# A segment-mean kernel: shorter look-ahead, a look in one slot, and a tail moved off GpSimd

## Chip, cores and metric

The kernel runs on one core of a Trainium2 chip. The metric is device time in microseconds, the median of several executions. The profile is one execution taken by the hardware profiler; its span is about 2 us shorter than the time.

## The reference

```python
def setup_inputs():
    n, num_segments = 10_000_000, 10000
    return {"data": np.random.randn(n).astype(np.float32),
            "segment_ids": np.sort(np.random.randint(0, num_segments, n))}

def reference(data, segment_ids):
    ...
    np.add.at(sums, segment_ids, data)
    np.add.at(counts, segment_ids, 1)
    return sums / np.maximum(counts, 1)
```

The ids are sorted, and a segment has about 1000 elements. The draw is fixed.

## The kernel before

Each of the 128 partitions takes 78125 consecutive elements, as 98 rows of 800. A row holds at most one segment boundary. For a group of four or five rows there is first a *look*: probes (every 160th id) tell the id at the start of each row (`V`), whether the row holds a boundary (`BT`), and where. A GpSimd gather fetches the 159 ids around the boundary, ScalarE adds them up, and that gives the exact split point `KK`. For every row ScalarE then forms the row's total `T` and VectorE the part before the split, `A` (the "split", one operation over 800 elements). `V`, `BT`, `KK`, `A` and `B` lie in one tile, which the profile calls `q_118` or `q`.

The program is written as slots: slot r issues the total and the split of row r, then whatever small work `put` has placed there, for a look (`first_look`, five steps) one step a slot. `X_PROBE`, `X_DATA`, `X_LOOK` and `X_SUM` are in rows ahead.

```python
X_PROBE = 18; X_DATA = 26; X_LOOK = 16; X_SUM = 7     # rows ahead
R1 = 94; R2 = NR + 4; C1 = 58; ON_ACT = 89

def first_look(g):                       # s1 to s5; s5 starts the gathers
    def s1():
        ...
        nc.vector.tensor_copy(out=V[:, a:e], in_=pr32[:, a:e, 0])

def keys(a, b):                          # s1: base1; s2: key = id - base; s3: dm
    def s2():
        nc.vector.tensor_scalar(out=KEY[:, PAD + a : PAD + b], in0=V[:, a:b],
            scalar1=base1[:, 0:1], scalar2=None, op0=ALU.subtract)

def windows_hold(r, n, o1, o2):          # part of the guard
    # s1, s2: j2 = (row - 1.625 - 1.25 * KEY) ** 2
    # s3: o1 = (j2 > 3.625**2) * BT      row with a boundary, outside its window
    ...

def verdict():                           # sum of all guard columns, over all partitions
    # s1: reduce, matmul with ones;  s2: badi = sum != 0

def finish():
    for f in sums(R1, R2, False): f()
    nc.vector.tensor_tensor(out=add[:, :, 0:m], in0=pk, in1=..FF.., op=ALU.mult)
    nc.vector.tensor_reduce(out=OUT[:, C1:NO], in_=add, axis=AX.X, op=ALU.add)
    ...  # four output DMAs
    with tc.If(verdict_reg[0] > 0):
        general_path(...)                # any sorted or unsorted ids, very slow

# the schedule (cut)
for g in range(HEAD, NG):
    put(max(bounds[g] - X_LOOK, 0), first_look(g))     # one step a slot
put(26, extend())
put(31, keys(0, 48))                                   # s2 in slot 32
put(36, ext_rows())
...
put(91, counts(66, R2), 3)
put(93, sums(66, R1), 4)
t, p = table(12, NT1 // 4, g), place(36, NO, g)        # g: on GpSimd
put(93, t[:1]); put(95, t[1:] + p[:1], 2); put(96, p[1:])
put(94, verdict())
after[96].append(lambda: verdict_reg.append(nc.values_load(badi[0:1, 0:1], ...)))
```

To turn rows into outputs, the kernel compares `KEY` (id - base) with column numbers, but only in windows of 12 rows for four columns, which fits ids that advance evenly. The guard tests that each boundary lies in its window. If one does not, the whole result is computed again by `general_path`, column by column. Rows from `R1` on skip the windows: they are compared with all columns from `C1` on and added by products (`pk`).

Of the kernel before, what the change touches and what calls it, by code (L numbers as in the profile page):

```python
# [9 lines left out]
FP32 = mybir.dt.float32  # L10
# [7 lines left out]
P = 128  # L18
# [8 lines left out]
NX = NR + E  # L27
BIG = float(1 << 24)
GROUPS = [4] + [5] * 18 + [4]
X_PROBE = 18  # L30
X_DATA = 26
X_LOOK = 16
X_SUM = 7
RING = 28
NO = 79
SHIFT = 6
ND = 2 * SHIFT + 1
NT1 = 92
R1 = 94
R2 = NR + 4  # L40
C1 = 58
ON_ACT = 89



# [68 lines left out]
def kernel(  # L114
# [116 lines left out]
    def first_look(g):  # L231

        a, b = bounds[g], bounds[g + 1]
        n = b - a
        eq = fpool.tile([P, n, K - 1], FP32, name="eq", bufs=3)
        jc = fpool.tile([P, n], FP32, name="jc", bufs=3)
        pos = fpool.tile([P, n], FP32, name="pos", bufs=3)
        last = b == NR

        def s1():  # L240
            if last:
                nc.vector.tensor_copy(out=pr32[:, NR - 1, 2 * (K - 1) : 2 * K], in_=snt32)
                nc.vector.tensor_copy(out=vend, in_=snt32[:, 0:1])
                nc.vector.tensor_copy(out=V[:, NR : NR + 1], in_=snt32[:, 0:1])
            in1b, in0b = bass.broadcast_tensor_aps(pr32[:, a:b, 0:1], pr32[:, a:b, 2 : 2 * K : 2])
            nc.vector.tensor_tensor(out=eq, in0=in0b, in1=in1b, op=ALU.is_equal)  # L246
            e = b if last else b + 1
            nc.vector.tensor_copy(out=V[:, a:e], in_=pr32[:, a:e, 0])  # L248

        def s2():  # L250
            nc.vector.tensor_reduce(out=jc, in_=eq, axis=AX.X, op=ALU.add)  # L251
            nc.vector.tensor_sub(out=BT[:, a:b], in0=V[:, a + 1 : b + 1], in1=V[:, a:b])  # L252

        def s3():
            nc.vector.tensor_scalar(  # L255
                out=ST[:, a:b], in0=jc, scalar1=float(S), scalar2=float(1 + W),
                op0=ALU.mult, op1=ALU.add,
            )
            nc.vector.tensor_scalar(  # L259
                out=NB[:, a:b], in0=BT[:, a:b], scalar1=1.0, scalar2=None, op0=ALU.not_equal  # L260
            )
            if last:
                nc.vector.tensor_scalar(
                    out=ST[:, NR - 1 : NR], in0=ST[:, NR - 1 : NR], scalar1=float(LAST), scalar2=None,
                    op0=ALU.min,
                )

        def s4():
            nc.vector.tensor_add(out=pos, in0=ST[:, a:b], in1=wb[:, a:b])  # L269
            nc.vector.scalar_tensor_tensor(  # L270
                out=QQ[:, a:b], in0=V[:, a:b], scalar=float(W), in1=ST[:, a:b],
                op0=ALU.mult, op1=ALU.add,
            )

        def s5():
            nc.vector.scalar_tensor_tensor(  # L276
                out=IDX[:, a:b], in0=NB[:, a:b], scalar=BIG, in1=pos, op0=ALU.mult, op1=ALU.add
            )

            nc.vector.scalar_tensor_tensor(  # L280
                out=QQ[:, a:b], in0=NB[:, a:b], scalar=-64.0 * BIG, in1=QQ[:, a:b], op0=ALU.mult,
                op1=ALU.add,
            )
            gather(g)

        return [s1, s2, s3, s4, s5]
# [16 lines left out]
        )  # L303

    def second_look(a, b):
        def s0():
            c = a
            while c < b:
                s = c % RING
                e = min(b, c - s + RING)  # L310
                nc.vector.tensor_reduce(  # L311
                    out=GS[:, c:e], in_=gt32[:, s : s + e - c, 0 : 2 * W : 2], axis=AX.X, op=ALU.add
                )
                c = e

        def s1():
            nc.vector.tensor_sub(out=KK[:, a:b], in0=QQ[:, a:b], in1=GS[:, a:b])  # L317

        def s2():
            nc.vector.tensor_mul(out=KK[:, a:b], in0=KK[:, a:b], in1=BT[:, a:b])  # L320

        return [s1] if a < ON_ACT else [s0, s1, s2]

    def total(r):
        n = min(L, D - r * L)
# [30 lines left out]
    KL = cpool.tile([P, R2 - R1], FP32, name="KL")  # L356
    pk = cpool.tile([P, NO - C1, R2 - R1], FP32, name="pk")
    add = cpool.tile([P, NO - C1, R2 - R1 + 1], FP32, name="add")
    OUT = cpool.tile([P, NO], FP32, name="OUT")
    nc.vector.memset(RF, 0.0)  # L360
    nc.vector.memset(CS[:, 0:1], 0.0)
# [14 lines left out]
    def view(ap, dims):  # L376
        return bass.AP(ap.tensor, ap.offset, [list(ap.ap[0])] + dims)
# [33 lines left out]
    def keys(a, b):  # L411
        def s1():
            if a == 0:
                nc.vector.tensor_add(out=base1, in0=V[:, 0:1], in1=pin)

        def s2():
            nc.vector.tensor_scalar(
                out=KEY[:, PAD + a : PAD + b], in0=V[:, a:b], scalar1=base1[:, 0:1], scalar2=None,
                op0=ALU.subtract,
            )  # L420
            if a == 0:
                nc.vector.tensor_sub(out=delta, in0=sp, in1=base1)

        def s3():
            if a == 0:
                nc.vector.tensor_scalar(
                    out=dm, in0=jj[:, 0:ND], scalar1=delta[:, 0:1], scalar2=None, op0=ALU.is_equal
                )

        return [s1, s2, s3]  # L430
# [137 lines left out]

        return [s1, s2, s3, s4, s5, s6, s7]

    def sums(a, b, weigh=True):
        def s1():
            c = min(b, NR)
            nc.vector.tensor_sub(out=B[:, a:c], in0=T[:, a:c], in1=A[:, a:c])  # L574

        def s2():
            nc.vector.tensor_tensor_scan(  # L577
                out=CS[:, a + 1 : b + 1], data0=NB[:, a:b], data1=B[:, a:b], initial=CS[:, a : a + 1],
                op0=ALU.mult, op1=ALU.add,
            )  # L580

        def s3():
            nc.vector.tensor_add(out=FF[:, a:b], in0=A[:, a:b], in1=CS[:, a:b])  # L583

        def s4():
            nc.vector.tensor_mul(out=RF[:, PAD + a : PAD + b], in0=FF[:, a:b], in1=RB[:, a:b])

        return [s1, s2, s3, s4] if weigh else [s1, s2, s3]
# [55 lines left out]
    def select(m0, m1, e):  # L644
        def s1():
            equal(e, sel[:, m0:m1], windows(KEY, m0, m1),
                  view(jj[:, 4 * m0 : 4 * m0 + 1], [[4, m1 - m0], [1, 4], [0, 12]]))

        return [s1]
# [33 lines left out]
    def pick():  # L683

        n, m = NO - C1, R2 - R1

        def s1():
            nc.gpsimd.tensor_scalar(
                out=KL, in0=V[:, R1:R2], scalar1=sp[:, 0:1], scalar2=None, op0=ALU.subtract
            )  # L690
            equal(nc.gpsimd, pk, view(KL[:, 0:1], [[0, n], [1, m]]),
                  view(jj[:, C1 : C1 + 1], [[1, n], [0, m]]))

        def s2():
            nc.gpsimd.tensor_tensor(  # L695
                out=pk, in0=pk, in1=view(RB[:, R1 : R1 + 1], [[0, n], [1, m]]), op=ALU.mult
            )

        return [s1, s2]

    def finish():
        n, m = NO - C1, R2 - R1
        for f in sums(R1, R2, False):
            f()
        nc.vector.tensor_tensor(
            out=add[:, :, 0:m], in0=pk, in1=view(FF[:, R1 : R1 + 1], [[0, n], [1, m]]), op=ALU.mult
        )
        nc.vector.tensor_reduce(out=OUT[:, C1:NO], in_=add, axis=AX.X, op=ALU.add)
        for i, (src, dst) in enumerate(own_outputs(OUT, out2d[0:1, :])):
            (nc.scalar if i % 2 else nc.sync).dma_start(out=dst, in_=src)  # L710
        with tc.If(verdict_reg[0] > 0):
            general_path(tc, fpool, ppool, data, segment_ids, out2d, iota)
# [11 lines left out]
    def put(r, steps, every=1):  # L724
        for i, f in enumerate(steps):
            after[r + i // every].append(f)
# [3 lines left out]
            after[-1].append(f)  # L730
    after[-1] += second_look(0, GROUPS[0])
    for a, b in zip(bounds[1:], bounds[2:]):
        put(a - 2 if a < ON_ACT else a - 3 if b < NR else a - 4, second_look(a, b))
    for g in range(HEAD, NG):
        put(max(bounds[g] - X_LOOK, 0), first_look(g))

    v, g = nc.vector, nc.gpsimd
    verdict_reg = []
# [8 lines left out]
    put(64, counts(48, 66), 2)  # L747
    put(67, sums(48, 66) + table(8, 12, v) + place(0, 36, v), 2)
    put(60, check(), 2)
    last_look = bounds[NG - 1] - X_LOOK + 4  # L750
    put(last_look + 1, keys(MID, NX)[1:] + check_late())
    put(last_look + 2, select(12, NT1 // 4, g))
    put(last_look + 2, pick()[:1])
    put(last_look + 2, [lambda: nc.sync.dma_start(out=out2d[0:SHIFT, :].rearrange("n u -> u n"), in_=tab[0:1, 0:SHIFT])])
    put(91, counts(66, R2), 3)
    put(93, pick()[1:])
    put(93, sums(66, R1), 4)
    t, p = table(12, NT1 // 4, g), place(36, NO, g)
    put(93, t[:1])
    put(95, t[1:] + p[:1], 2)  # L760
    put(96, p[1:])
    put(94, verdict())
    after[96].append(lambda: verdict_reg.append(nc.values_load(badi[0:1, 0:1], min_val=0, max_val=1)))
    assert max(after) <= NR - 1

    pnext = 0
# [62 lines left out]
```

## Time and profile before

| | before |
|---|---|
| time, median of 3 | 197.04 us |
| last data landed (the trace's DMA packet records) | 178.0 us |
| VectorE starts the split of row 84, its last wait for data | 165.22 us |
| VectorE's last operation ends | 188.94 us |
| end of the span | 194.885 us |

Here are three parts of the page of the kernel before: the span, the busy time of each engine, and the busy tenths in 40 slices of 4.9 us.

```profile
span 194.9 us, 1624 instructions
PE 1.6 (1%) x6; PEld 1.4 (1%) x6; DVE 139.9 (72%) x541; ACT 138.1 (71%) x393; POOL 108.0 (55%) x121
...
DVE  6535197874775867495967686967999679899960
DMA  6999999999999999999999999999999999993000
```

The DMA queues are full until about 178 us. After that VectorE (DVE) works off a backlog. The last slices hold only the output and the end of the program. The split of row 84 is the last at which VectorE waits for data (columns as explained below):

```profile
165.22 1.05 DVE L333 SCALAR_TENSOR_TENSOR junk_v<-iota,q_118,data_t 128x800 bf16<-128x800 f32 x1 [0.46 <-DMA data_t<-in_data_dram]
```

The timeline shows the end of the kernel before. Columns: start in us, duration in us, engine, line, operation, output <- inputs; in brackets the idle time before it and what ended it.

```profile
169.17 0.98 DVE L311 TENSOR_REDUCE GS<-GT 128x5 f32<-128x795 int32 x1 [0.47 <-ACT junk_a L300]
175.20 0.82 DVE L311 TENSOR_REDUCE GS<-GT 128x4 f32<-128x636 int32 x1
184.44 0.15 DVE L528 TENSOR_SCALAR badi<-badp 128x1 int32<-128x1 f32 x1
184.60 1.33 POOL L668 TENSOR_TENSOR shf<-tab,dm 128x559 f32<-128x559 f32 x1 [1.45 <-DVE badi L528]
185.96 0.45 DVE L675 TENSOR_REDUCE OUT<-shf 128x22 f32<-128x286 f32 x1 [0.41 <-POOL shf L668]
188.59 0.35 DVE L708 TENSOR_REDUCE OUT<-add 128x21 f32<-128x189 f32 x1
188.97 1.48 SPq L710 DMA_DIRECT2D out_dram<-OUT  x2
```

The first two operations add up the gathered ids of rows 89 to 97 a second time: ScalarE has 98 such sums in the page, one for every row. The last GpSimd operation (POOL) ends at 185.9 us. VectorE is done at 188.94 us, and the span ends 5.95 us later.

### The profile page before, as it was taken

Reading aid. Unit: us, or ns where it says so; the run is one execution under the profiler, and the core shown is the slowest. Engines: PE = TensorE matmul, PEld = TensorE weight load, DVE = VectorE, ACT = ScalarE, POOL = GpSimd, SP = SyncE. Lnnn points to the kernel's source line nnn. Section 1 sums busy time; section 2 is a strip of 40 time slices with the busy share of each in tenths; the row PEclk is TensorE's granted clock in tenths of the full one; section 3 lists DMA queues with packets and bytes.
Section 4 is the critical chain, followed back from the end, with each engine's and each line's share of the span. In section 5 each row is a group of like instructions: output and inputs, shape, how many; then the busy total and the mean of one; then the engine's idle time right before and its main releaser. Section 6 shows DMA issues by size and latency. Waiting matters only on the chain.

```text
span 194.9 us, 1624 instructions
## 1 busy us (share of the span) xinstructions
PE 1.6 (1%) x6; PEld 1.4 (1%) x6; DVE 139.9 (72%) x541; ACT 138.1 (71%) x393; POOL 108.0 (55%) x121
## 2 busy tenths in 40 slices
PE   0000000000000200000000000000000000000100
PEld 0000000000000100000000000000000000000100
DVE  6535197874775867495967686967999679899960
ACT  0043398985999998595968686866978779999310
POOL 5487737775467573746456373737383674850410
DMA  6999999999999999999999999999999999993000
GB/s 82 127 107 323 244 400 246 385 246 403 202 336 318 372 246 260 360 279 345 176 389 252 367 210 405 238 317 264 380 261 274 396 401 400 399 403 133 2 2 9
DMA packets 75141, 53.40 MB, mean 274 GB/s; under 512 B 65601, under 2 KB 65684, under 8 KB 75127
## 3 DMA queue, kind: packets, MB, share of 16 engines
q1 hardware_dynamic: 70251, 40.54, 73.9%
q0 software_dynamic: 4704, 12.74, 21.7%
q14 instruction: 14, 0.11, 0.2%
q10 hardware_dynamic: 172, 0.00, 0.1%
HBM read 56.46 MB, written 0.04 MB: 290 GB/s over the span
## 4 chain that ended last, share of the span: by engine, by line
DMA 31%; SPq 30%; issue 14%; DVE 10%; ACT 10%; POOL 3%; POOLq 0%; DVEq 0%; ACTq 0%
SPq L162 24%; DMA data_t<-in_data_dram 23%; DMA GT<-in_segment_ids_dram,IDX 7%; SPq L154 6%; ACT junk_a L328 5%; DVE junk_v L333 5%; ACT junk_a L300 4%; POOL GT L290 2%; POOL shf L668 1%; DVE CS L577 1%; DVE tab L658 0%; DVE GS L311 0%; DVE ct L559 0%; DVE FF L583 0%; DVE q_118 L574 0%
## 5 line engine op out<-in xcount | busy, mean ns | idle before, releaser
L290 POOL DMA_INDIRECT GT<-in_segment_ids_dram,IDX x98 | 98.3, 1003 | 66.2 <-ACT junk_a L300 31.2
L333 DVE SCALAR_TENSOR_TENSOR junk_v<-iota,q_118,data_t 128x800 bf16<-128x800 f32 x98 | 102.1, 1042 | 26.8 <-DMA data_t<-in_data_dram 23.7
L328 ACT ACTIVATE junk_a<-data_t 128x800 bf16<-128x800 f32 x98 | 85.0, 867 | 22.5 <-DMA data_t<-in_data_dram 13.6
L300 ACT ACTIVATE junk_a<-GT 128x159 bf16<-128x159 int32 x98 | 34.0, 346 | 15.6 <-DMA GT<-in_segment_ids_dram,IDX 8.3
L300 ACT ACTIVATION_READ_ACCUMULATOR junk_a<-GT 128x1 f32 x98 | 18.3, 187 | 0.0
L328 ACT ACTIVATION_READ_ACCUMULATOR junk_a<-data_t 128x1 f32 x98 | 18.2, 186 | 0.0
L317 DVE TENSOR_TENSOR q_118<-QQ,GS 128x5 f32<-128x5 f32 (+1 forms) x20 | 3.2, 160 | 15.9 <-issue 11.6
L300 ACT ACT_TABLE_LOAD x1 | 1.3, 1283 | 9.6 <-DVE q_118 L252 9.6
L333 DVE DVE_READ_ACCUMULATOR junk_v<-iota,q_118,data_t 128x1 f32 x98 | 8.1, 83 | 0.0
L246 DVE TENSOR_TENSOR eq<-pr 128x20 f32<-128x20 int32 (+1 forms) x20 | 3.5, 175 | 2.6 <-DMA pr<-in_segment_ids_dram 2.6
L695 POOL TENSOR_TENSOR pk<-pk,RB 128x168 f32<-128x168 f32 x1 | 0.5, 507 | 7.2 <-DVE q_118 L574 7.2
L248 DVE CAST q_118<-pr 128x6 f32<-128x6 int32 (+2 forms) x20 | 3.7, 183 | 0.0
L259 DVE TENSOR_SCALAR NB<-q_118 128x5 f32<-128x5 f32 (+1 forms) x20 | 3.5, 176 | 0.0
L255 DVE TENSOR_SCALAR ST<-jc 128x5 f32<-128x5 f32 (+1 forms) x20 | 3.5, 174 | 0.0
L251 DVE TENSOR_REDUCE jc<-eq 128x5 f32<-128x20 f32 (+1 forms) x20 | 3.4, 171 | 0.0
L269 DVE TENSOR_TENSOR pos<-ST,wb 128x5 f32<-128x5 f32 (+1 forms) x20 | 3.3, 167 | 0.0
L276 DVE SCALAR_TENSOR_TENSOR IDX<-NB,pos 128x5 int32<-128x5 f32 (+1 forms) x20 | 3.2, 158 | 0.0
L280 DVE SCALAR_TENSOR_TENSOR QQ<-NB,QQ 128x5 f32<-128x5 f32 (+1 forms) x20 | 3.1, 157 | 0.0
L270 DVE SCALAR_TENSOR_TENSOR QQ<-q_118,ST 128x5 f32<-128x5 f32 (+1 forms) x20 | 3.1, 156 | 0.0
L252 DVE TENSOR_TENSOR q_118<-q_118 128x5 f32<-128x5 f32 (+1 forms) x20 | 3.1, 156 | 0.0
L311 DVE TENSOR_REDUCE GS<-GT 128x5 f32<-128x795 int32 (+1 forms) x2 | 1.8, 899 | 0.6 <-ACT junk_a L300 0.5
L668 POOL TENSOR_TENSOR shf<-tab,dm 128x559 f32<-128x559 f32 x1 | 1.3, 1332 | 1.4 <-DVE badi L528 1.4
(110 smaller groups left out, 41.8 us busy)
## 6 DMA issues: line engine op xcount, KB each, us to landing
data_t<-in_data_dram SPq DMA_DIRECT2D x48, 800.0 KB
GT<-in_segment_ids_dram,IDX POOLq DMA_INDIRECT x98
pr<-in_segment_ids_dram SPq DMA_DIRECT2D x18, 25.0 KB
data_t<-in_data_dram SPq DMA_DIRECT2D x1, 400.0 KB
data_t<-in_data_dram SPq DMA_DIRECT2D x1, 262.5 KB
out_dram<-OUT SPq DMA_DIRECT2D x1, 36.6 KB
pr<-in_segment_ids_dram SPq DMA_DIRECT2D x1, 21.0 KB
pr<-in_segment_ids_dram SPq DMA_DIRECT2D x1, 18.0 KB
```

Of the source, the lines that this page charges most:

```text
L154: nc.sync.dma_start(out=pr_flat[:, a:b], in_=ids_p[:, a * S : (b - 1) * S + 1 : S])
L162: nc.sync.dma_start(out=d[:, 0 : c - a], in_=data_p[:, a:c])
L246: nc.vector.tensor_tensor(out=eq, in0=in0b, in1=in1b, op=ALU.is_equal)
L248: nc.vector.tensor_copy(out=V[:, a:e], in_=pr32[:, a:e, 0])
L251: nc.vector.tensor_reduce(out=jc, in_=eq, axis=AX.X, op=ALU.add)
L255: nc.vector.tensor_scalar(out=ST[:, a:b], in0=jc, scalar1=float(S), scalar2=float(1 + W), op0=ALU.mult, op1=ALU.add,)
L259: nc.vector.tensor_scalar(out=NB[:, a:b], in0=BT[:, a:b], scalar1=1.0, scalar2=None, op0=ALU.not_equal)
L269: nc.vector.tensor_add(out=pos, in0=ST[:, a:b], in1=wb[:, a:b])
L290: nc.gpsimd.indirect_dma_start(out=GT[:, r % RING, :], out_offset=None, in_=ids2d[:], in_offset=bass.IndirectOffsetOnAxis(ap=IDX[:, r : r ...
L300: nc.scalar.activation(out=junk_a[:, 0:W], in_=gt32[:, r % RING, 0 : 2 * W : 2], func=ACT.Relu, accum_out=GS[:, r : r + 1],)
L328: nc.scalar.activation(out=junk_a[:, 0:n], in_=d, func=ACT.Copy, accum_out=t)
L333: nc.vector.scalar_tensor_tensor(out=junk_v[:, 0:n], in0=iota[:, 0:n], scalar=KK[:, r : r + 1], in1=d, op0=ALU.is_lt, op1=ALU.mult, accum_ ...
```

## The change

The intent is to look later, so that fewer probes come before the first data, to take the second summing and the closing products off VectorE's end, and to let GpSimd finish early. Its core (cut: helper bodies and some schedule lines are left out):

```diff
-X_PROBE = 18
+X_PROBE = 13
-X_LOOK = 16
-X_SUM = 7
+X_LOOK = 11
+X_SUM = 6
-R1 = 94
+R1 = 84
-C1 = 58
-ON_ACT = 89
+C1 = 50
@@ second_look: the tensor_reduce over GT and the product with BT are gone @@
@@ pick: product with RB on VectorE; wq = sum of the last columns; wp = pk[last row] - wq @@
@@ all_but_last (new): sums, product and reduction of rows 84.. without the last row @@
@@ finish @@
+        nc.vector.scalar_tensor_tensor(
+            out=most, in0=wq, scalar=T[:, r : r + 1], in1=most, op0=ALU.mult, op1=ALU.add)
+        nc.vector.scalar_tensor_tensor(
+            out=OUT[:, C1:NO], in0=wp, scalar=A[:, r : r + 1], in1=most, op0=ALU.mult, op1=ALU.add)
@@ schedule @@
-        put(max(bounds[g] - X_LOOK, 0), first_look(g))
+        put(max(bounds[g] - X_LOOK, 0), first_look(g), 5)
-    put(last_look + 2, select(12, NT1 // 4, g))
+    put(last_look + 2, select(12, NT1 // 4, v))
-    put(91, counts(66, R2), 3)
-    put(93, sums(66, R1), 4)
-    t, p = table(12, NT1 // 4, g), place(36, NO, g)
-    put(94, verdict())
+    put(R1, counts(66, R1), 4)
+    put(R1 + 2, sums(66, R1), 4)
+    t, p = table(12, NT1 // 4, v), place(36, NO, g)
+    put(R1 + 3, t + p[:1])
+    put(R1 + 4, verdict())          # read at slot R1 + 6
+    put(NR - 4, counts(R1, R2), 4)
+    put(NR - 3, pick()[1:], 2)
+    put(NR - 2, all_but_last(), 5)
```

More of the change, by code (lines that the diff above doesn't have):

```diff
@@ L305, in second_look @@
     def second_look(a, b):
-        def s0():
-            c = a
-            while c < b:
-                s = c % RING
-                e = min(b, c - s + RING)
-                nc.vector.tensor_reduce(
-                    out=GS[:, c:e], in_=gt32[:, s : s + e - c, 0 : 2 * W : 2], axis=AX.X, op=ALU.add
-                )
-                c = e
         def s1():
             nc.vector.tensor_sub(out=KK[:, a:b], in0=QQ[:, a:b], in1=GS[:, a:b])
-        def s2():
-            nc.vector.tensor_mul(out=KK[:, a:b], in0=KK[:, a:b], in1=BT[:, a:b])
-        return [s1] if a < ON_ACT else [s0, s1, s2]
+        return [s1]
     def total(r):
@@ L358 @@
     add = cpool.tile([P, NO - C1, R2 - R1 + 1], FP32, name="add")
+    wq = cpool.tile([P, NO - C1], FP32, name="wq")
+    wp = cpool.tile([P, NO - C1], FP32, name="wp")
+    most = cpool.tile([P, NO - C1], FP32, name="most")
     OUT = cpool.tile([P, NO], FP32, name="OUT")
@@ L569, in counts, with sums @@
         return [s1, s2, s3, s4, s5, s6, s7]
-    def sums(a, b, weigh=True):
+    def sums(a, b, weigh=True, upto=NR):
         def s1():
-            c = min(b, NR)
+            c = min(b, upto)
             nc.vector.tensor_sub(out=B[:, a:c], in0=T[:, a:c], in1=A[:, a:c])
@@ L694, in s2, with s3, s4, all_but_last @@
         def s2():
-            nc.gpsimd.tensor_tensor(
+            nc.vector.tensor_tensor(
                 out=pk, in0=pk, in1=view(RB[:, R1 : R1 + 1], [[0, n], [1, m]]), op=ALU.mult
             )
-        return [s1, s2]
-    def finish():
-        n, m = NO - C1, R2 - R1
-        for f in sums(R1, R2, False):
-            f()
-        nc.vector.tensor_tensor(
-            out=add[:, :, 0:m], in0=pk, in1=view(FF[:, R1 : R1 + 1], [[0, n], [1, m]]), op=ALU.mult
-        )
-        nc.vector.tensor_reduce(out=OUT[:, C1:NO], in_=add, axis=AX.X, op=ALU.add)
+        def s3():
+            nc.vector.tensor_reduce(out=wq, in_=pk[:, :, NR - R1 : m], axis=AX.X, op=ALU.add)
+        def s4():
+            nc.vector.tensor_sub(out=wp, in0=pk[:, :, NR - 1 - R1], in1=wq)
+        return [s1, s2, s3, s4]
+    def all_but_last():
+        n, m = NO - C1, R2 - R1
+        def s4():
+            nc.vector.tensor_tensor(
+                out=add[:, :, 0:m], in0=pk, in1=view(FF[:, R1 : R1 + 1], [[0, n], [1, m]]), op=ALU.mult
+            )
+        def s5():
+            nc.vector.tensor_reduce(out=most, in_=add, axis=AX.X, op=ALU.add)
+        return sums(R1, R2, False, NR - 1) + [s4, s5]
+    def finish():
+        r = NR - 1
+        nc.vector.scalar_tensor_tensor(
+            out=most, in0=wq, scalar=T[:, r : r + 1], in1=most, op0=ALU.mult, op1=ALU.add
+        )
+        nc.vector.scalar_tensor_tensor(
+            out=OUT[:, C1:NO], in0=wp, scalar=A[:, r : r + 1], in1=most, op0=ALU.mult, op1=ALU.add
+        )
         for i, (src, dst) in enumerate(own_outputs(OUT, out2d[0:1, :])):
@@ L732 @@
     for a, b in zip(bounds[1:], bounds[2:]):
-        put(a - 2 if a < ON_ACT else a - 3 if b < NR else a - 4, second_look(a, b))
+        put(a - 1, second_look(a, b))
     for g in range(HEAD, NG):
-        put(max(bounds[g] - X_LOOK, 0), first_look(g))
+        put(max(bounds[g] - X_LOOK, 0), first_look(g), 5)
     v, g = nc.vector, nc.gpsimd
@@ L749 @@
     put(60, check(), 2)
-    last_look = bounds[NG - 1] - X_LOOK + 4
-    put(last_look + 1, keys(MID, NX)[1:] + check_late())
-    put(last_look + 2, select(12, NT1 // 4, g))
-    put(last_look + 2, pick()[:1])
-    put(last_look + 2, [lambda: nc.sync.dma_start(out=out2d[0:SHIFT, :].rearrange("n u -> u n"), in_=tab[0:1, 0:SHIFT])])
-    put(91, counts(66, R2), 3)
-    put(93, pick()[1:])
-    put(93, sums(66, R1), 4)
-    t, p = table(12, NT1 // 4, g), place(36, NO, g)
-    put(93, t[:1])
-    put(95, t[1:] + p[:1], 2)
-    put(96, p[1:])
-    put(94, verdict())
-    after[96].append(lambda: verdict_reg.append(nc.values_load(badi[0:1, 0:1], min_val=0, max_val=1)))
+    last_look = bounds[NG - 1] - X_LOOK
+    put(last_look + 1, keys(MID, NX)[1:2] + check_late(), 3)
+    put(last_look + 1, pick()[:1])
+    put(last_look + 2, select(12, NT1 // 4, v))
[3 more added lines that the diff above has]
+    put(R1 + 3, t + p[:1])
+    put(R1 + 6, p[1:])
+    put(R1 + 1, [lambda: nc.sync.dma_start(out=out2d[0:SHIFT, :].rearrange("n u -> u n"), in_=tab[0:1, 0:SHIFT])])
+    put(R1 + 4, verdict())
+    after[R1 + 6].append(lambda: verdict_reg.append(nc.values_load(badi[0:1, 0:1], min_val=0, max_val=1)))
+    put(NR - 4, counts(R1, R2), 4)
+    put(NR - 3, pick()[1:], 2)
+    put(NR - 2, all_but_last(), 5)
     assert max(after) <= NR - 1
```

## The prediction

> **What bounds the kernel.** Until about 178 us it is the DMA queues: in the windows view of 5 us stretches the DMA share is about 1.0 in nearly every stretch from 5 to 175 us, alternating between about 400 GB/s (data, gathers) and about 240 GB/s (probe bursts). In the trace's DMA packet records the probe bursts of one group take 2.5 to 3.5 us; the last one ends at 150.4 us; the last data rows (96, 97) land at 177.4 and 178.1 us. The change loads the same bytes, so I expect the last landing unmoved, within 1 us.
>
> After that comes a VectorE backlog. In the timeline VectorE waits for data last at row 84 (starts 165.22; its packets landed 163.27). From there to its last reduction (ends 188.94) it is almost continuously busy: 14 splits at 1.09 us apart make 15.2 us, the rest is small work between them, some waits, and 1.5 us of closing chain. About 6 us follow for the output DMA and the end. ScalarE ends its last total at 185.96, held 3.1 us by the verdict register; it is not the limit.
>
> **What the change does.**
> - Head: with probes 13 ahead, one probe group fewer (about 2.7 us) goes before the second data tile, so rows up to about 80 land some 2 us earlier. But the last probe group now lies before row 82 instead of row 76. From row 82 on the order is as before: nothing gained at the end.
> - First look in one slot: ten dependent operations take 1.12 us (seen in the head, 10.37 to 11.49) against about 0.5 us when spread in pairs. Absorbed in the middle by VectorE's data waits (23.7 us in the waits view), but the look at slot 83 delays row 84 by about 0.5 us.
> - Removed from VectorE's tail: two gather reductions (0.98 and 0.82 us), two small products, some waits (0.5 us for ScalarE, 0.4 us for GpSimd), most of the closing chain (1.5 to about 0.4 us).
> - Added: comparison and product over 528 elements moved from GpSimd (estimate 0.70 us each: 384 elements took 0.55). The Trainium skill, "VectorE: DVE Perf Modes", the errata section, gives (N+151)/0.96 ns for an fp32 tensor_tensor, and the 0.55 us agree. The pick over 29x18 = 522 elements instead of 168: product with the counts 0.70 (GpSimd's before), product with the sums 0.70 instead of 0.34, reduction 0.72 instead of 0.35; counts and sums cut in two, about 10 more chained operations of 0.1 to 0.2 us.
>
> Sum of non-split VectorE work from row 84 to the end: about 8.8 us before including waits, about 10.1 after by my slot-by-slot count. All of it lies on the critical path, since the data for rows 86 to 97 come faster (about 1.0 us a row) than VectorE takes them. So VectorE ends 1.3 to 2.3 us later; the output part is unchanged.
>
> **Predicted: 198.8 us, range 196.2 to 201.2.** Faster by over 2%: 0.05; within 2%: 0.85; slower by over 2%: 0.10.
>
> **What would show it.** Right: last data landing at 177 to 178.5 us; VectorE without data waits after about row 84; more than 9 us of non-split VectorE work after row 84; closing chain after the last split under 0.6 us; GpSimd's last work before 180 us; ScalarE's last total before VectorE's end. Wrong: the last landing moves by over 2 us; VectorE waits for data at rows above 90; or ScalarE waits for gathers grow in the tail, because the look, and so the gather, now comes later.
>
> **What would make it wrong.** If small operations hide better between splits than I count, the tail is shorter and the kernel wins 1 to 2 us. If later gathers stall ScalarE, or the register read stalls it at row 90, it loses more.

## The result

The changed kernel took 194 320 us (median of 4, 194 316 to 194 321), against 197.03 us for the kernel before in the same runs. The result was correct. The ratio is 983 (95% interval 978 to 988). Here and below a ratio is the mean time of one kernel's fast runs over that of the other's fast runs of the same rounds, so it is not quite the ratio of the medians. An execution over 1.5% above the fastest of its kernel counts as slow and is left out.

The page of the changed kernel, with the same parts and its two costliest groups (line, engine, operation, output <- inputs, count | busy us, mean ns | idle before):

```profile
span 194318.1 us, 1698540 instructions
PE 89056.3 (46%) x156256; PEld 26546.7 (14%) x156256; DVE 73210.8 (38%) x253055; ACT 138.1 (0%) x393; POOL 104.9 (0%) x117
...
L87 PE MATMUL g_prod<-g_ol,g_oh 128*79 128x256 f32 x156250 | 89054.7, 674 | 105080.1 <-DVE g_ol L84 105080.1
L78 DVE TENSOR_SCALAR g_oh<-iota,g_hi 128x79 f32<-128x79 f32 x78125 | 23408.1, 300 | 96177.0 <-PE g_prod L87 77069.8
```

Nearly all time is in tiles named `g_`, which only the general path has: 78125 columns, one after another. The verdict was not zero. The timeline of the changed kernel shows that the fast path ran to its end before that:

```profile
189.74 0.24 DVE L712 SCALAR_TENSOR_TENSOR most<-wq,T,most 128x29 f32<-128x29 f32 x1
190.02 0.25 DVE L715 SCALAR_TENSOR_TENSOR OUT<-wp,q,most 128x29 f32<-128x29 f32 x1
190.27 0.27 DVE L54 MEMSET g_acc<- 79x256 f32 x1
190.29 1.49 SPq L719 DMA_DIRECT2D out_dram<-OUT  x2
192.48 0.39 SPq L61 DMA_DIRECT2D g_i<-in_segment_ids_dram  x1
```

Two questions follow. Why did the guard fire, and what is the change worth without that?

### The profile page after: what moved, and what is told of

The parts are those of the page before. It is cut to its first block, busy times and chain, and to the rows that moved or that the text cites. A ratio compares the mean times of both kernels' runs of the same rounds, so it can differ in the third digit from the quotient of the medians.

```text
span 194318.1 us, 1698540 instructions
## 1 busy us (share of the span) xinstructions
PE 89056.3 (46%) x156256; PEld 26546.7 (14%) x156256; DVE 73210.8 (38%) x253055; ACT 138.1 (0%) x393; POOL 104.9 (0%) x117
## 5 line engine op out<-in xcount | busy, mean ns | idle before, releaser
L87 PE MATMUL g_prod<-g_ol,g_oh 128*79 128x256 f32 x156250 | 89054.7, 674 | 105080.1 <-DVE g_ol L84 105080.1
L78 DVE TENSOR_SCALAR g_oh<-iota,g_hi 128x79 f32<-128x79 f32 x78125 | 23408.1, 300 | 96177.0 <-PE g_prod L87 77069.8
L87 PEld LDWEIGHTS g_prod<-g_ol,g_oh 128*79 128x79 f32 x156250 | 26545.3, 232 | 167588.9 <-DVE g_ol L84 167588.9
L81 DVE TENSOR_SCALAR g_ol<-iota,g_lo 128x128 f32<-128x128 f32 x78125 | 26673.1, 341 | 0.0
L84 DVE TENSOR_SCALAR g_ol<-g_ol,g_dat 128x128 f32<-128x128 f32 x78125 | 22384.5, 287 | 2739.2
L88 DVE TENSOR_TENSOR g_acc<-g_acc,g_prod 79x256 f32<-79x256 f32 x15625 | 6518.0, 417 | 19255.5 <-PE g_prod L87 19255.5
L319 DVE SCALAR_TENSOR_TENSOR junk_v<-iota,q,data_t 128x800 bf16<-128x800 f32 x98 | 102.3, 1044 | 26.4 <-DMA data_t<-in_data_dram 25.2
```

Of the source, the lines that this page charges most:

```text
L78: nc.vector.tensor_scalar(out=oh, in0=ramp[:, 0:HI], scalar1=hi[:, at], scalar2=None, op0=ALU.is_equal)
L81: nc.vector.tensor_scalar(out=ol[:, 0:LO], in0=ramp[:, 0:LO], scalar1=lo[:, at], scalar2=None, op0=ALU.is_equal)
L84: nc.vector.tensor_scalar(out=ol[:, LO : 2 * LO], in0=ol[:, 0:LO], scalar1=dat[:, at], scalar2=None, op0=ALU.mult)
L87: nc.tensor.matmul(out=prod, lhsT=oh, rhs=ol, start=u == 0, stop=u == U - 1)
L88: nc.vector.tensor_add(out=acc, in0=acc, in1=prod)
L319: nc.vector.scalar_tensor_tensor(out=junk_v[:, 0:n], in0=iota[:, 0:n], scalar=KK[:, r : r + 1], in1=d, op0=ALU.is_lt, op1=ALU.mult, accum_ ...
```

## The experiments

### Why the guard fired

The input does not break any condition of the guard: computed on the host, no boundary lies outside its window, and row 84 clears column 50 by 11 in the tightest partition. So some value in the kernel had to be wrong. The trace shows an order that has changed. First the kernel before: the operation at L248 copies the start ids of a group into `V`, the one at L417 forms the keys of rows 0 to 47. The copy shown is that of rows 44 to 48 (slot 28).

```profile
67.24 0.16 DVE L248 CAST q_118<-pr 128x6 f32<-128x6 int32 x1
...
75.31 0.24 DVE L417 TENSOR_SCALAR KEY<-q_118,base_130 128x48 f32<-128x48 f32 x1
```

The same two operations in the changed kernel, L406 and L247:

```profile
72.39 0.40 DVE L406 TENSOR_SCALAR KEY<-q,base 128x48 f32<-128x48 f32 x1
73.66 0.17 DVE L245 TENSOR_TENSOR eq<-pr 128x20 f32<-128x20 int32 x1
73.75 0.16 DVE L247 CAST q<-pr 128x6 f32<-128x6 int32 x1
```

The look at rows 44 to 48 has moved from slot 28 to slot 33, because 44 - 11 = 33. The keys stayed in slot 32, a number written by hand. (Row 44 itself is known earlier, as the end of the group before.) So the keys of rows 45 to 47 are formed from the zeros with which the tile starts. This is no race between engines: both operations run on VectorE, in the order of the program, and read initialised memory. Only the order is wrong.

Theory A: this order alone fires the guard. Theory B: the guard's new comparison (row 84, column 50) fails. Theory C: the verdict register is read too early, or the alarm is false.

**Keys two slots later.**

```diff
-    put(31, keys(0, 48))
+    put(33, keys(0, 48))
```

> The changed kernel with one number different: the keys of rows 0 to 47 are formed at slots 33 to 35 instead of 31 to 33, so their subtraction (slot 34) comes after the look at rows 44 to 48 (slot 33). Theory A (the keys were formed from boundary values not yet written, the guard saw rows 45 to 47 as out of their windows and the general path ran): the verdict is 0, no general path, 198.4 us (VectorE's last operation was at 190.3 us in the changed kernel against 188.9 before, so 197.0 + 1.4), result correct. Theory B (the guard's new comparison with row 84 and column 50 fails) or C (the verdict register is read too early): still about 194 300 us.

Measured: correct, 195.74 us (six runs, 194.78 to 196.94), ratio to before 0.993 (0.988 to 0.998), so a little faster, by less than 1%. There was no general path. The timeline of this kernel has the copy before the keys again:

```profile
73.72 0.17 DVE L247 CAST q<-pr 128x6 f32<-128x6 int32 x1
75.74 0.24 DVE L406 TENSOR_SCALAR KEY<-q,base 128x48 f32<-128x48 f32 x1
```

Theory A holds. The time is 2.7 us under the expected 198.4, which is the subject of the next part. This kernel is called "the mended change" below.

**The same fault put into the kernel before.**

```diff
-    put(31, keys(0, 48))
+    put(26, keys(0, 48))
```

> The kernel before with the keys of rows 0 to 47 formed at slots 26 to 28 instead of 31 to 33: their subtraction (slot 27) then precedes the look at rows 44 to 48 (slot 28), the same fault without anything else of the change. Theory A: the general path runs, about 194 300 us, result correct. Theories B and C: nothing happens, about 197 us.

Measured: correct, 194 337 us. The fault needs nothing else of the change.

**The guard's row-84 comparison taken out of the changed kernel.**

```diff
-                out=bad[:, 2 * n : 2 * n + 1], in0=sp, scalar=float(C1), in1=V[:, R1 : R1 + 1],
+                out=bad[:, 2 * n : 2 * n + 1], in0=sp, scalar=-1.0e6, in1=V[:, R1 : R1 + 1],
```

> The changed kernel with the guard's comparison of row 84 with column 50 made always true (a constant far below). Theory A: no change, about 194 300 us, result correct. Theory B: about 198 us.

Measured: correct, 194 339 us. Theory B falls.

**The verdict forced to zero (wrong).**

```diff
-            nc.vector.tensor_scalar(out=badi, in0=badp, scalar1=0.0, scalar2=None, op0=ALU.not_equal)
+            nc.vector.tensor_scalar(out=badi, in0=badp, scalar1=-1.0, scalar2=None, op0=ALU.is_lt)
```

> The changed kernel with the verdict forced to 0 (the sum compared with below -1, which it never is), keys as in the change: wrong on purpose. Theory A: 198.4 us, the same as with the keys formed later, within 0.5 us, and a wrong result: by a count on the host from the input, 305 segment boundaries lie in rows 45 to 47 of the 128 partitions, so some 305 of the 10000 outputs should be wrong. Theory C (a correct verdict read too early, or a false alarm): about 198.4 us and a correct result.

Measured: 195.09 us and a wrong result, relative error 0.16540031. I then took the reference's output on the host and set to zero exactly the 305 outputs whose segments end in rows 45 to 47: the relative error is 0.16540031. So the fast path lost those 305 outputs and no others, and the guard was right. Theory C falls.

**One row more of lead.**

```diff
-X_PROBE = 13
-X_LOOK = 11
+X_PROBE = 14
+X_LOOK = 12
```

> The changed kernel with the look 12 rows ahead instead of 11 (probes 14 instead of 13), keys at slots 31 to 33 as in the change: the look at rows 44 to 48 then falls into slot 32, the slot of the keys' subtraction, and is put into it first. Theory A: one row of lead is the whole difference: no general path, 195 to 197 us, result correct. If any other part of the change set the guard off, still about 194 300 us.

Measured: correct, 194.88 us (one run). The look at rows 44 to 48 then falls into slot 32, ahead of the keys:

```profile
73.69 0.17 DVE L247 CAST q<-pr 128x6 f32<-128x6 int32 x1
74.62 0.24 DVE L406 TENSOR_SCALAR KEY<-q,base 128x48 f32<-128x48 f32 x1
```

One row of look-ahead separates 195 us from 194 ms.

### What the change is worth once mended

By my count VectorE should end later and the kernel be slower. The mended change has VectorE's last operation at 189.96 us, 1.0 us later than before, yet its span ends at 193.94 us, 0.95 us earlier. From VectorE's last operation to the end it takes 3.98 us instead of 5.95. Its last wait for data, its row 84 and its last operation:

```profile
160.62 1.05 DVE L319 SCALAR_TENSOR_TENSOR junk_v<-iota,q,data_t 128x800 bf16<-128x800 f32 x1 [1.47 <-DMA data_t<-in_data_dram]
...
164.11 1.04 DVE L319 SCALAR_TENSOR_TENSOR junk_v<-iota,q,data_t 128x800 bf16<-128x800 f32 x1
...
189.71 0.25 DVE L715 SCALAR_TENSOR_TENSOR OUT<-wp,q,most 128x29 f32<-128x29 f32 x1
```

The profile page does not count the closing instructions as busy; the trace has them. Each engine closes the program with an instruction called DRAIN. These are the records of GpSimd at the end (start, duration, in us); "SyncE's own end" is the end of SyncE's DRAIN before the engines meet:

```
before             TENSOR_TENSOR 184.60 1.33   TENSOR_LOAD (verdict) 184.62 0.50   COMPARE_BRANCH 185.18 0.04
                   DRAIN 185.62 8.41  -> 194.03;   SyncE's own end 192.09
mended change      TENSOR_TENSOR 174.95 1.34   TENSOR_LOAD (verdict) 176.07 0.49   COMPARE_BRANCH 176.62 0.05
                   DRAIN 177.09 8.16  -> 185.24;   SyncE's own end 193.11
```

Theory D: GpSimd's closing DRAIN takes about 8.2 us, and the program ends about 0.85 us after the later of it and SyncE's end. In the kernel before that was GpSimd. Theory E: the output DMA sets the end, and the shorter close has another cause.

**A GpSimd copy that waits for the pick weights.**

```diff
+    late = cpool.tile([P, 1], FP32, name="late")
+    put(NR - 2, [lambda: nc.gpsimd.tensor_copy(out=late, in_=wp[:, 0:1])])
     put(NR - 2, all_but_last(), 5)
```

> The changed kernel with the keys formed later, plus one 128x1 copy on GpSimd that waits for the pick weights (about 186.7 us) and whose result nobody uses. Theory D (GpSimd's closing DRAIN takes about 8.2 us after its last work, and the program ends at the later of that and SyncE's end): GpSimd's DRAIN ends near 195 us, the span is 195.7 us against 193.9 without the copy, the time some 1.8 us longer than with the keys formed later alone. Theory E (the end is set by the output DMA alone and the shorter close has another cause): no change, within 0.3 us.

Measured: 195.67 us, ratio 0.994 (0.988 to 0.999), not longer than the mended change. The profile does show the mechanism: DRAIN from 184.97 to 193.13, SyncE done at 190.91, and 6.23 us from VectorE's last operation to the end. But in that execution the loads ended at 174.1 us, 2.7 us earlier than in the mended change's. The effect is of the size of the differences between runs, so by time this test is inconclusive: the 1.8 us that theory D had forecast did not show.

**The last GpSimd product moved to VectorE, in the kernel before.**

```diff
-    t, p = table(12, NT1 // 4, g), place(36, NO, g)
+    t, p = table(12, NT1 // 4, g), place(36, NO, v)
```

> The kernel before with its last GpSimd product (placing columns 36 to 78, 1.33 us at 184.6) moved to VectorE, where it should cost 0.74 us less the 0.41 us that VectorE waited for it. Theory D: GpSimd's last work ends near 183.2, its DRAIN at 191.4; the program then ends by SyncE, 3.1 us after VectorE's last operation (189.3), so a span near 193.2 and a time about 1.6 us (0.8 percent) below the kernel before. Theory E: VectorE ends 0.3 us later, so the time is 0.3 us longer.

Measured: 197.69 us, ratio 1.001 (0.997 to 1.004). My expectation (1.6 us faster by theory D, 0.3 us slower by E) failed both ways. The trace says why: GpSimd's last product ended at 183.3, but it then waited to read the verdict (185.5), and its DRAIN ran from 186.57 to 194.73. So the DRAIN comes in its turn after the last instruction of any kind, a register read and the branch on it included.

**A GpSimd copy that waits for the very last operation.**

```diff
+        late = cpool.tile([P, 1], FP32, name="late")
+        nc.gpsimd.tensor_copy(out=late, in_=OUT[:, NO - 1 : NO])
         for i, (src, dst) in enumerate(own_outputs(OUT, out2d[0:1, :])):
```

> The changed kernel with the keys formed later, plus one 128x1 copy on GpSimd that waits for VectorE's very last operation (the copy that waited for the pick weights came only 3 us before it, in a run whose loads ended 2.7 us earlier, and moved the end by about as much as the runs differ). Theory D (GpSimd's DRAIN takes 8.2 us after its last instruction and the program ends 0.85 us after it): GpSimd's DRAIN starts about 0.5 us and ends 8.7 us after VectorE's last operation, and from that operation to the end of the span it is 9.5 us instead of 3.9; the time is about 5.5 us longer, near 201 us, a ratio of 1.02 to the kernel before instead of 0.99. Theory E (the output DMA sets the end): 195.7 us.

Measured: correct, 199.94 us, ratio 1.012 (1.005 to 1.019). Its timeline ends with

```profile
187.95 0.25 DVE L715 SCALAR_TENSOR_TENSOR OUT<-wp,q,most 128x29 f32<-128x29 f32 x1
188.22 1.49 SPq L721 DMA_DIRECT2D out_dram<-OUT  x2
188.26 0.18 POOL L719 COPY late<-OUT 128x1 f32<-128x1 f32 x1 [13.74 <-DVEq L722]
```

and after the copy of 0.18 us come a DRAIN from 188.70 to 196.86 and the end at 197.71 us: 9.51 us after VectorE's last operation, as theory D said, where SyncE was done at 191.35. One 128x1 copy in the wrong place costs about 4 us of time (5.5 were expected; in this profile the loads ended 1.7 us earlier than in the mended change's). Theory D holds and E falls. What the DRAIN does in its 8 us no run shows.

**The kernel before with GpSimd released early, nothing else.**

```diff
-    t, p = table(12, NT1 // 4, g), place(36, NO, g)
-    put(94, verdict())
-    after[96].append(...)
+    t, p = table(12, NT1 // 4, g), place(36, NO, v)
+    put(90, verdict())
+    after[92].append(...)
```

> The kernel before with only GpSimd released early: verdict at slots 90 to 92 instead of 94 to 96, last GpSimd product on VectorE. (Moving the product alone gained nothing: GpSimd still had to read the verdict at 185.5 us, and its DRAIN began only after that.) Theory D: VectorE's last operation 0.3 us later, the stretch from it to the end of the span 3.9 us instead of 5.95, so about 1.7 us (0.9 percent) faster than before, 195.4 us. Theory E: 0.3 us slower.

Measured: 197.20 us, ratio 0.999 (0.995 to 1.004); the 195.4 us of theory D were missed. The close did shrink to 3.98 us. But from the last landing to VectorE's last operation it took 12.16 us instead of 10.91. Part of that is the product that VectorE took over (0.74 us, less the 0.41 us that it had waited for GpSimd's). Part is a wait of 0.28 us that was not there before: ScalarE, which also reads the verdict, now reads it while it still has totals to form, and VectorE waits for a total at row 93:

```profile
182.42 0.41 DVE L574 TENSOR_TENSOR q<-T,q 128x28 f32<-128x28 f32 x1 [0.28 <-ACT junk_a L328]
```

The rest of the 1.25 us is not accounted for, and the loads also ended 0.7 us later in that execution. Released early in this way, GpSimd brought no gain that could be measured.

**The kernel before without the second summing of ids, first try.**

```diff
-ON_ACT = 89
+ON_ACT = 1000
-        put(a - 2 if a < ON_ACT else a - 3 if b < NR else a - 4, second_look(a, b))
+        put(a - 2, second_look(a, b))
```

> The kernel before without the two VectorE reductions that sum the gathered ids of rows 89 to 97 a second time (ScalarE had summed them), and without the two small products that went with them: this part of the change alone. VectorE's tail should end 2.4 to 2.8 us earlier, at 186.1 to 186.5, and GpSimd's last product with it, at about 183.3. Under theory D the end is then still set by GpSimd's DRAIN (191.5), span 192.4 us, time 194.6 us; under theory E 194.3 to 194.6 us as well.

Measured: 195.08 us, but a wrong result (relative error 0.126). This was the same kind of fault: the split points of rows 94 to 97 now come in slot 92, while `counts` reads them in slot 91. The guard does not see it, since it tests keys and boundaries, not split points.

**The same, mended.**

```diff
+        put(a - 2 if b < NR else a - 3, second_look(a, b))
```

> The part run before, mended (its wrong result came from my own slip: the last rows' split points were formed one slot after the counts that use them): the kernel before without the second summing of rows 89 to 97 on VectorE. Result correct; VectorE's last operation near 186.9 where the loads end at 177.5, GpSimd's DRAIN ends near 192, time 195.0 us (the wrong kernel had 195.1), ratio 0.988.

Measured: correct, 195.30 us, ratio 0.991 (0.985 to 0.997). VectorE's backlog after the last landing is 9.58 us instead of 10.91. The close is still 5.94 us, set by GpSimd's DRAIN (to 192.75).

**Without the second summing, and GpSimd released early.** This is the kernel just above with the diff of "GpSimd released early".

> The same with GpSimd released early as well: the verdict formed and read at slots 90 to 92 instead of 94 to 96, and the last GpSimd product (placing, 1.33 us) on VectorE. Theory D: GpSimd's last work is the table product near 181.2, its DRAIN ends near 190, SyncE near 190.4 (3.1 us after VectorE's last operation at 187.2), so the span is about 191.3 and the time 193.3 us, 1.7 us under the kernel without the second summing alone. Theory E: 0.3 us over it.

Measured: correct, 194.05 us (six runs, 193.25 to 194.72), ratio 0.983 (0.978 to 0.987). Backlog 10.15 us, close 3.98 us. Theory D had forecast 193.3. This kernel has the lowest ratio so far, and it keeps the old distances of probes and looks. Its interval overlaps that of the kernel just above, so what the early release adds is shown by the close (3.98 instead of 5.94 us) more than by the time.

### What stays open: the end of the loads

The loads ended at 176.2 us on average in eight profiles of the changed kernel and its near variants, the repeat below included (174.1 to 178.1), and at 177.7 us in seven of the kernel before and its variants with the old distances (176.8 to 178.7). The 176.8 is that of the kernel before with early keys, and on its chip three variants of the changed kernel landed at 176.7 to 178.1; the profiles come from several chips. Theory F: the nearer probes cause it. Theory G: it is chance of the run. Three more runs were made side by side, on one chip.

> The changed kernel with the keys formed later once more, beside the next two on the same chip: 195.7 us, last landing 174 to 178 us, from the last landing to VectorE's last operation 13.1 us, from there to the end 3.98 us.

Measured: 194.97 us, ratio 0.992 (0.987 to 0.997); last landing 175.9, backlog 13.08, close 3.98 us. It repeats the first run of the mended change.

```diff
 # mended change with
-X_PROBE = 13
-X_LOOK = 11
+X_PROBE = 17
+X_LOOK = 15
-        put(max(bounds[g] - X_LOOK, 0), first_look(g), 5)
+        put(max(bounds[g] - X_LOOK, 0), first_look(g))
-    last_look = bounds[NG - 1] - X_LOOK
+    last_look = bounds[NG - 1] - X_LOOK + 4
```

> The same with the look in five slots again, 15 rows ahead, and the probes 17 ahead (the last steps of a look fall into the same slot as in the change). Theory F (the near probes make the loads end earlier): last landing near 177.9 us as in the kernel before, VectorE's backlog 0.5 us shorter than 13.1 since the look before row 84 is spread again, so about 1 us slower than the mended change in the same job. Theory G (the earlier landings are chance of the run): last landing in the same range as the repeat, and 0.5 us faster.

Measured: 195.78 us, ratio 0.995 (0.990 to 1.000); last landing 177.2, backlog 11.92 us. The backlog is 1.2 us shorter and the landing 1.3 us later. This leans to F, but the intervals of the two ratios overlap, and the run changes two things, the distances and the spreading of the look.

```diff
 # fastest kernel so far with
-X_PROBE = 18
-X_LOOK = 16
-X_SUM = 7
+X_PROBE = 13
+X_LOOK = 11
+X_SUM = 6
 # looks in one slot, keys in slots 33 to 35, second looks one row later, verdict one slot later
```

> The fastest kernel so far (the kernel before without the second summing, GpSimd released early: 194.05 us, last landing 177.3, backlog 10.15, close 3.98) with the change's probes 13 and look 11 ahead in one slot, keys formed later. Theory F: last landing about 1.5 us earlier, backlog up by 0.5 us, so about 193 us. Theory G: 0.5 us slower than 194.05.

Measured: correct, 193.70 us, ratio 0.985 (0.980 to 0.990), not to be told from 0.983. Its last landing, 177.0, is only 0.3 us before that of the kernel with the old distances, which speaks against F, though the two profiles are from different chips. Its backlog grew to 12.58 us, mostly by one wait, because the sum of the last ids now comes too late for the counts:

```profile
176.23 0.16 DVE L317 TENSOR_TENSOR q<-QQ,GS 128x4 f32<-128x4 f32 x1 [1.70 <-ACT junk_a L300]
```

Whether the probe distance moves the end of the loads stays open. What is steady is the work behind it: from the start of row 84's split to VectorE's last operation it takes 25.8 us in seven of the eight profiles above of the changed kernel and its near variants (25.2 us with 12 rows of look), without a wait for data. So VectorE's end there differs between executions only as row 84's start does, from 161.9 to 165.4 us.

### The sums

All values in us from one profile each, the ratios from all fast runs; backlog is from the last landing to the end of VectorE's last operation, close from there to the end of the span. The three add up to the span.

| kernel | last landing | backlog | close | what sets the end | ratio to before |
|---|---|---|---|---|---|
| before | 178.0 | 10.91 | 5.95 | GpSimd DRAIN | 1 |
| mended change | 176.8 | 13.13 | 3.98 | SyncE | 0.993 |
| mended change, GpSimd copy at the end | 175.1 | 13.06 | 9.51 | GpSimd DRAIN | 1.012 |
| before, GpSimd early | 178.7 | 12.16 | 3.98 | SyncE | 0.999 |
| before, no second summing | 178.1 | 9.58 | 5.94 | GpSimd DRAIN | 0.991 |
| both of these | 177.3 | 10.15 | 3.98 | SyncE | 0.983 |

## Why the prediction was wrong

- **The step that failed** is silent in the prediction: it took for granted that the changed kernel stays on the fast path. It costed "Head" and "First look in one slot" as times only, and "What would make it wrong" names small operations and stalls, no change of result. The look's slot fell from 28 to 33 for rows 44 to 48 while their reader stayed in slot 32. The measured price is 194 ms instead of 195.7 us. Everything needed to see it was in the diff and the code.
- **"The output part is unchanged", "about 6 us follow for the output DMA and the end": wrong.** Of the 5.95 us only 3.98 belong to the output and SyncE. The rest was GpSimd's 8.4 us DRAIN sticking out, and the change took it away (the run with the copy after the very last operation shows the mechanism). This alone does not make the mended change faster (0.993) instead of slower by the predicted 0.9%: in the two profiles the close gives 1.97 us, the backlog takes 2.22, so the two about cancel, and the 0.95 us by which the span is shorter come with a landing 1.20 us earlier, whose cause is open. Its times, 195.74 and 194.97 us, lie below the predicted 198.8 and, in the median, below the lower limit 196.2 too.
- **VectorE's tail: right in kind, its growth counted too small.** Predicted was an end 1.3 to 2.3 us later, with the last landing unmoved. Between before and the mended change the backlog grew by 2.2 us; the end itself came only 1.0 us later, since row 84's split started 1.1 us earlier (164.11 against 165.22). The non-split work from row 84 on is 10.9 us (from 164.11 to 189.96 us, less 13 splits at 1.09 and the last at 0.76), where the prediction had 10.1; the kernel before has 8.8 in the same count, so the growth was 2.1 us where 1.3 had been counted.
- **Closing chain, waits, GpSimd: right.** After the last split 0.53 us follow (under 0.6 predicted); VectorE does not wait for data after row 84; GpSimd's last work ends at 176.3 (before 180); ScalarE's last total comes before VectorE's end.
- **Last landing "unmoved, within 1 us": not settled.** It was 1.2 us earlier in the mended change's profile and 1.5 us earlier on average over the family, with a spread of 4 us; the runs meant to explain it disagree.
- **Formula used: right.** The Trainium skill, "VectorE: DVE Perf Modes", section on the TRN2 errata, gives (N+151)/0.96 ns; for 528 elements that is an estimate of 0.71 us, and the comparison and the product measured 0.69 and 0.70 us in the changed kernel. Its page "GPSIMD Engine Reference", section "Engine selection", puts two-input elementwise work at about twice VectorE's time; the product over 528 elements took 1.23 us on GpSimd before and 0.70 us on VectorE after, 1.76 times.

## What to carry to other kernels

When a look-ahead distance changes, list every reader of what the look writes and compare slots, above all readers whose slot is a literal number: an order error on one engine is no race between engines, and here nothing but the guard saw it. A guard with a slow fallback turns such an error into a correct result at a thousandfold time, so ask first whether the fast path is still taken. Before costing the tail, find which engine's last instruction sets the end of the program: here GpSimd needed some 8 us to close, so its last work, register reads included, had to come about 5.4 us before VectorE's end (0.4 us to the DRAIN and its 8.16 us, less the 3.2 us by which SyncE's own end follows VectorE's).

## What the Trainium skill lacked or had wrong

- "VectorE: DVE Perf Modes", section "The DRAIN you can't avoid", describes the boilerplate DRAIN as about 12 ns, constant, on all five engines. Here GpSimd's closing DRAIN took 8.16 us where nothing was in flight before it, and 8.35 to 8.91 us where it began while the last operation still ran; SyncE's took 7 ns, VectorE's 17 ns and ScalarE's 138 ns in the kernel before. There GpSimd's set the end of the program. These records carry a line of the program (L824), so they may not be the runtime's own that the page means; whether they are, no run shows.
- No page that I found gives the length of such a closing DRAIN on GpSimd, or says that a late register read and branch hold it back; in the run with only the last product moved it began at 186.57 us, 3.3 us after GpSimd's last product and 0.4 us after its branch.
